# Conv module of a two-layer trunk: nine convolution blocks on TensorE, grouped layer-norm statistics, an ordered layer norm, and a queue of their own for the modulations' loads

## The chip, the cores and the metric

One core of one Trainium2 chip. The metric is the device time of one execution in microseconds, as the median of several runs. PE is TensorE, DVE VectorE, ACT ScalarE, POOL GpSimd, SP SyncE, which only issues transfers here.

## What is computed

A residual stream x of 256 tokens by 2048 goes through two layers. Layer 0 has a convolution module as its token mixer, layer 1 gated linear attention; each layer then has a feed-forward part with a short convolution. Every part is wrapped in norms and in shift, scale and gate that a product of the conditioning vector c with a 2048 x 12288 matrix gives ("modulations", adaLN):

```python
c_act = silu(c)
for i in range(2):
    shift_m, scale_m, gate_m, shift_f, scale_f, gate_f = split(c_act @ ada_w[i] + ada_b[i])
    h = rms_norm(x, norm_g[i, 0]) * (1 + scale_m) + shift_m
    y = conv_module(h) if i == 0 else gla(h)
    x = x + gate_m * rms_norm(y, norm_g[i, 1])
    h = rms_norm(x, norm_g[i, 2]) * (1 + scale_f) + shift_f
    x = x + gate_f * rms_norm(conv_ffn(h), norm_g[i, 3])

def conv_module(h):
    a, gate = split(h @ w_in)                       # 2048 -> 2 x 2048
    z = causal_dwconv(a * sigmoid(gate), dw_w) + dw_b   # 31 taps, each channel by itself
    z = silu(layer_norm(z, ln_g, ln_b))             # over the 2048 channels
    return z @ w_out
```

The change lies in layer 0's convolution module, the "first stage".

## The kernel before

All large products are taken in a split form: a weight block's high part is a cast on ACT (L121), its low part a subtraction on DVE (L123), and PE takes three products (high by high, low by high, high by low). Weights come as tiles of 1 MiB ("raw"), by a class `Stream`: a list of items in a fixed order, loaded ahead on SP's queue (`load`, L92 to L99) into a pool of four buffers. The adaLN items of layer 0 that are marked early go through a second pool of four buffers, `cols`, but in the same list and the same queue, so that a load whose buffer is still in use holds up all that stand behind it on SP.

An adaLN item is of one of two kinds. A *column* item goes to PE (`ada_col`): 512 of the inputs against 512 of the outputs, four narrow products a tile (L364) into an accumulator `ada`; when it is full, DVE transposes it (L371) and PE sums the four partial rows (`adas`, L378), and DVE adds the bias (L381). A *row* item goes to DVE (`ada_row`, L350): one multiply-and-reduce of a 128 x 2048 tile with the vector `cb`, about 2.28 us.

The first stage (`conv_mixer`, L597 on) runs in four parts.

- *Start.* The tokens x, the vector and the parameters `pr` are loaded, the shift and scale of the first norm come as column items of half width ("adah"), and the normed tokens are transposed.
- *cin.* The 16 blocks of 128 channels of a and of gate, in six steps (L742 to L762, products L756 to L758), 32 weight items. `gather` (L658) makes a * sigmoid(gate) of a block and puts it into one of two lists.
- *Convolution.* Eight blocks go to DVE (`taps_dve`, 30 instructions a block, L685), and eight to PE (PE_BLOCKS, `taps_pe`): 16 narrow products `ps_late` (L713) that shift the block, four copies on ACT (L715), and 32 narrow products `ps_conv` (L730) with diagonal matrices `zt` that DVE (L724, half of them) and ACT (the other half) build. As a block is finished it enters the layer norm's statistics: a product with a 128 x 128 matrix of ones for the mean (`mean_add`, L644), and, once 12 blocks give a first mean, its squares less that mean (L631, L632) by another such product (`squares`, L633). The rest of cin and the column items lie between these.
- *Layer norm and cout.* From the statistics DVE and ACT make the mean `mu` and 1/deviation `r_ln` (L778 to L786); every block is centered (L789), multiplied (L792), passed through silu (L793) and split (L424, L425) into `uc`. cout then takes 2048 columns in four blocks of 512: 96 products each (L522 to L524), the gate's multiplication (`y`, L583) at each block's end. Between its products stand column items, and between its low parts row items, by two tables (COLS_COUT, ROWS_COUT: how many at each weight item). The gate goes through DRAM to be spread over the partitions: `gate_rows` writes 2048 single numbers (`row`, L508) and reads them back four times (`gs`, L512), on POOL's queue.

The order of instructions on each engine is fixed when the program is built: the framework's scheduler places an instruction when its inputs are expected, by priorities, and an engine then runs its list in order. The change moves many instructions on all engines in the first stage; from the feed-forward part of layer 0 on the order stays.

Of the kernel before, what the change touches and what calls it, by code (L numbers as in the profile page):

```python
# [13 lines left out]
P = 128  # L14
# [13 lines left out]
PE_BLOCKS = (5, 7, 9, 11, 12, 13, 14, 15)  # L28
# [6 lines left out]
COLS_CONV = 16  # L35
# [11 lines left out]
COLS_COUT = (0, 0, 0, 1), (1, 1, 1, 1), (1, 1, 0, 0), (0, 0, 0, 0)  # L47
# [6 lines left out]
C_TAP = C_AB + 2 * 6 * KT  # L54
C_DWB = C_TAP
# [9 lines left out]
class Stream:  # L65
# [26 lines left out]
    def load(self, upto):  # L92
        while self.loaded < min(upto, len(self.items)):
            it = self.items[self.loaded]
            pool = self.cols if it["early"] else self.raw
            r = pool.tile([P, 2048], F32, tag="raw", name=f"raw{self.loaded}")
            self.nc.sync.dma_start(out=r[:, : it["n"]], in_=it["src"])
            self.raws[self.loaded] = r
            self.loaded += 1  # L99
# [91 lines left out]
def trunk_kernel(ctx: ExitStack, tc: tile.TileContext, x, cvec, ccol, adar, adac, adah, par, taps, wgate,  # L191
# [14 lines left out]
    nc.sync.dma_start(out=cc, in_=ccol)  # L206
    ones = const.tile([P, P], F32, tag="ones", name="ones")
# [4 lines left out]
    G.memset(onec, 1.0)  # L212

# [4 lines left out]
    pr = const.tile([P, NPAR], F32, tag="pr", name="pr")  # L218
# [70 lines left out]
    early_cols = list(cols[:COLS_CONV])  # L289
    fillc(COLS_CONV)  # L290
# [55 lines left out]

    def ada_row(key, r):

        _, l, m, k = key
        V.tensor_tensor_reduce(out=r, in0=r, in1=cb, scale=1.0, scalar=0.0, op0=ALU.mult, op1=ALU.add,  # L350
                               accum_out=mod[l, m][:, k : k + 1])

    def ada_col(key, r):
# [8 lines left out]
        for j in range(per):  # L362
            kt = per * i + j
            nc.tensor.matmul(ps[32 * (j % 4) : 32 * (j % 4) + 32], cz[:, kt], r[:, j * n : (j + 1) * n],  # L364
                             start=kt < 4, stop=kt >= KT - 4, tile_position=(0, 32 * (j % 4)))
        if i == KT // per - 1:

            trs = []
            for h in range(0, n, T):
                tr = small.tile([P, T], F32, tag="sq", name=f"adat{l}{m}{k0}{h}", bufs=3)  # L370
                V.transpose(out=tr, in_=ps[:, h : h + T])  # L371
                trs.append(tr.rearrange("p (c a i) -> p c a i", a=4, i=32))

            def sums():
                pt = apool["sums"](f"adas{l}{m}{k0}")
                for c, tr in enumerate(trs):
                    for a in range(4):
                        nc.tensor.matmul(pt[32 * a : 32 * a + 32, 2 * c : 2 * c + 2], mask32, tr[:, :, a, 0],  # L378
                                         start=True, stop=True, tile_position=(0, 32 * a))
# [122 lines left out]
    def gate_rows(l, which, gate, room=None):  # L502
# [4 lines left out]
        with nc.allow_non_contiguous_dma("2048 numbers"):  # L507
            G.dma_start(out=row.rearrange("k p -> p k"), in_=mod[l, gate])  # L508
        gs = []
        for c in range(4):  # L510
            g = room[c].rearrange("p (a b) -> p a b", b=P) if room else hpool.tile([P, 4, P], F32, tag="h", name=f"g{l}{which}{c}")
            G.dma_start(out=g, in_=row[4 * c : 4 * c + 4].unsqueeze(0).to_broadcast([P, 4, P]))  # L512
# [3 lines left out]
    def token_products(pv, t, parts, act, kt, nk):  # L516
# [7 lines left out]
        nc.tensor.matmul(pv, al, wh, start=False, stop=kt == nk - 1)  # L524
# [47 lines left out]
    def proj_out(name, act, l, which, gate, room=None):  # L572
        ss = new_sums(f"y{l}{which}")
        ys, dg, gs = {}, {}, []
        for c in range(4):

            def each(t, pv):
                if not gs:
                    gs.extend(gate_rows(l, which, gate, room))
# [17 lines left out]
    def conv_mixer(l):  # L597
        with early as cx:
            st.ahead = 8
            cm = cx.enter_context(tc.tile_pool(name="cm", bufs=2))  # L600
            tp = cm.tile([P, KT * (CW + 32)], F32, tag="tp", name="tp", bufs=1)
# [8 lines left out]
            on_dve, on_pe, ready, order = [], [], [], []  # L610
# [14 lines left out]

            def squares(j):
                n = len(squared)
                if n == 0:
                    acc["v"] = psum1.tile([P, T], F32, tag="acc", name="acc_v")
                sq = small.tile([P, T], F32, tag="sq", name=f"sq{j}", bufs=3)  # L630
                V.tensor_sub(sq, zs[j], mean_a)  # L631
                A.activation(sq, sq, AF.Square)  # L632
                nc.tensor.matmul(acc["v"], ones, sq, start=n == 0, stop=n == KT - 1)  # L633
                squared.append(j)
# [3 lines left out]
            def mean_add(j):  # L638


                n = len(added)
                if n in (0, NA):
                    acc["m"] = (psum1 if n == 0 else pp["ps"]).tile([P, 2 * T], F32, tag="acc" if n == 0 else "ps", name=f"acc_m{n}")[:, :T]
                nc.tensor.matmul(acc["m"], ones, zs[j], start=n in (0, NA), stop=n in (NA - 1, KT - 1))  # L644
                added.append(j)
                if n == NA - 1:
                    A.activation(mean_a, acc["m"], AF.Copy, scale=1.0 / (NA * P))
                    V.tensor_scalar_mul(part_a, mean_a, NA / KT - 1.0)
                if n >= NA - 1:
                    for i in added[len(squared) :]:  # L650
                        squares(i)

            def tap(j, s):

                c = j * CW + CW - 1 - s
                return tp[:, c : c + 1]

            def gather(j, ps, last):  # L658
# [7 lines left out]
                if last:  # L666
# [5 lines left out]
                    if j in PE_BLOCKS:  # L672
                        on_pe.append((j, zp, z))
# [27 lines left out]
            def taps_pe():  # L701


                while on_pe:
                    j, zc, z = on_pe.pop(0)
# [12 lines left out]
                    c0 = KT * CW + j * 32  # L718
                    w = tp[:, c0 : c0 + 32].rearrange("p (j a) -> p a j", a=8)
# [13 lines left out]
                    A.activation(z, ps, AF.Identity, bias=pc(C_DWB + j))  # L733
# [6 lines left out]
            A.dma_start(out=cb, in_=cvec.to_broadcast([P, D]))  # L740
# [23 lines left out]
            for step in range(1000):  # L764
                if step < len(early_cols):
# [372 lines left out]
```

## Time and profile before

| | us |
|---|---|
| runs | 2373.4, 2375.62, 2379.9 (median 2375.62) |
| profiled execution | 2376.87 |
| its span | 2375.2 |
| PE busy in the span | 2318.7 |
| first cin product | 29.6 |
| last product of the layer norm's statistics | 352.3 |
| first cout product | 368.8 |
| end of cout's third column block | 440.7 |
| mean granted clock of PE | 0.992 |

A row of a table of windows gives start and end, the busy us of PE, of its weight loads (PEld), of DVE, ACT and POOL with the number of instructions, the clock granted to PE as a share of full speed, the mean busy share of the 16 DMA engines, and GB/s. A row of the timeline gives start, duration, engine, line, operation, output and input, and in brackets how long the engine stood idle before and what it waited for. A row of a grouped list gives the count, busy us in total, and ns of one. A row of waits gives us in total, times, longest.

### The profile page before, as it was taken

Reading aid. Unit: us, or ns where it says so; the run is one execution under the profiler, and the core shown is the slowest. Engines: PE = TensorE matmul, PEld = TensorE weight load, DVE = VectorE, ACT = ScalarE, POOL = GpSimd, SP = SyncE. Lnnn points to the kernel's source line nnn. Section 1 sums busy time; section 2 is a strip of 40 time slices with the busy share of each in tenths; the row PEclk is TensorE's granted clock in tenths of the full one; section 3 lists DMA queues with packets and bytes.
Section 4 is the critical chain, followed back from the end, with each engine's and each line's share of the span. In section 5 each row is a group of like instructions: output and inputs, shape, how many; then the busy total and the mean of one; then the engine's idle time right before and its main releaser. Section 6 shows DMA issues by size and latency. Waiting matters only on the chain.

```text
span 2375.2 us, 34238 instructions
## 1 busy us (share of the span) xinstructions
PE 2318.7 (98%) x13516; PEld 1955.8 (82%) x13516; DVE 1772.2 (75%) x2554; ACT 1212.4 (51%) x1909; POOL 16.8 (1%) x43
## 2 busy tenths in 40 slices
PE   6999998999999999999999999999999999999998
PEld 5888746788878888888878888888888888888886
DVE  3779998778878888888877877756887466645665
ACT  5334465555534554345565576655554455544543
POOL 0000000000000000000000000000000000000000
PEclk9999998999999999999999999999999999999999
DMA  9878778657799878988946756563778555555553
GB/s 387 344 311 322 299 222 309 265 216 276 291 310 348 303 279 316 362 288 298 345 174 258 283 216 227 168 227 121 286 280 275 193 190 193 189 185 196 193 199 121
DMA packets 86577, 609.30 MB, mean 257 GB/s; under 512 B 10064, under 2 KB 10128, under 8 KB 13456
## 3 DMA queue, kind: packets, MB, share of 16 engines
q1 hardware_dynamic: 84800, 601.84, 69.2%
q0 software_dynamic: 1472, 4.23, 0.6%
q8 instruction: 106, 1.74, 0.3%
q10 hardware_dynamic: 144, 1.05, 0.1%
q14 instruction: 55, 0.45, 0.1%
HBM read 604.94 MB, written 2.13 MB: 256 GB/s over the span
## 4 chain that ended last, share of the span: by engine, by line
PE 95%; DMA 2%; DVE 1%; ACT 1%; issue 0%; SPq 0%; DVEq 0%; ACTq 0%
PE ps_fb L410 14%; PE ps_fa L410 14%; PE ps_fa L412 7%; PE ps_fb L412 7%; PE ps_fo L524 7%; PE ps_fo L523 7%; PE ps_fo L522 6%; PE ps_cin L756 3%; PE ps_cin L758 3%; PE ps_r L410 2%; PE ps_cin L757 2%; PE ada L364 2%; PE ps_r L412 1%; PE ps_q L410 1%; PE ps_cout L522 1%; PE ps_k L410 1%
## 5 line engine op out<-in xcount | busy, mean ns | idle before, releaser
L123 DVE TENSOR_TENSOR lo<-raw,hi 128x1024 fp32r<-128x1024 f32 (+1 forms) x760 | 914.3, 1214 | 398.7 <-ACT hi L121 395.5
L121 ACT CAST hi<-raw 128x1024 fp32r<-128x1024 f32 (+1 forms) x760 | 784.9, 1042 | 807.4 <-PE ps_fa L410 195.4
L410 PE MATMUL ps_fa<-h,hi 128*128 128x512 f32 x1408 | 356.4, 393 | 0.4 <-ACT hn L486 0.4
L410 PE MATMUL ps_fb<-h,hi 128*128 128x512 f32 x1408 | 354.9, 392 | 0.0
L350 DVE CUSTOM_DVE_ANT_0 raw<-raw,cb 128x2048 f32<-128x2048 f32 x140 | 319.6, 2284 | 30.6 <-DMA raw<-in_adar 30.5
L410 PEld LDWEIGHTS ps_fa<-h,hi 128*128 128x128 f32 x1408 | 252.9, 189 | 45.7 <-DVE h L488 0.6
L410 PEld LDWEIGHTS ps_fb<-h,hi 128*128 128x128 f32 x1408 | 252.5, 189 | 44.2
L523 PE MATMUL ps_fo<-lo,u 128*128 128x512 f32 x704 | 274.6, 390 | 4.1 <-DVE lo L123 4.1
L524 PE MATMUL ps_fo<-hi,u 128*128 128x512 f32 x704 | 274.6, 390 | 0.0
L522 PE MATMUL ps_fo<-hi,u 128*128 128x512 f32 x704 | 273.7, 390 | 0.0
L412 PEld LDWEIGHTS ps_fa<-h,lo 128*128 128x128 f32 x1408 | 193.7, 190 | 15.1 <-DVE lo L123 0.5
L412 PEld LDWEIGHTS ps_fb<-h,lo 128*128 128x128 f32 x1408 | 193.7, 190 | 14.7
L412 PE MATMUL ps_fa<-h,lo 128*128 128x256 f32 x1408 | 198.3, 282 | 0.1
L412 PE MATMUL ps_fb<-h,lo 128*128 128x256 f32 x1408 | 198.2, 282 | 0.0
L523 PEld LDWEIGHTS ps_fo<-lo,u 128*128 128x128 f32 x704 | 132.6, 188 | 32.1 <-DVE lo L123 4.6
L756 PE MATMUL ps_cin<-h,hi 128*128 128x256 f32 x512 | 148.4, 293 | 7.3 <-ACT hi L121 7.2
L524 PEld LDWEIGHTS ps_fo<-hi,u 128*128 128x128 f32 x704 | 132.5, 188 | 27.7
L522 PEld LDWEIGHTS ps_fo<-hi,u 128*128 128x128 f32 x704 | 132.6, 188 | 27.1
L758 PE MATMUL ps_cin<-h,lo 128*128 128x256 f32 x512 | 145.2, 288 | 1.1 <-DVE lo L123 1.1
L757 PE MATMUL ps_cin<-h,hi 128*128 128x256 f32 x512 | 146.0, 287 | 0.0
L756 PEld LDWEIGHTS ps_cin<-h,hi 128*128 128x128 f32 x512 | 100.0, 196 | 21.5 <-ACT hi L121 11.8
L758 PEld LDWEIGHTS ps_cin<-h,lo 128*128 128x128 f32 x512 | 99.2, 196 | 3.2 <-issue 1.7
(240 smaller groups left out, 2697.9 us busy)
## 6 DMA issues: line engine op xcount, KB each, us to landing
raw<-in_fin SPq DMA_DIRECT2D x176, 1024.0 KB, 4.8
raw<-in_adar SPq DMA_DIRECT2D x140, 1024.0 KB, 5.6
raw<-in_fout SPq DMA_DIRECT2D x88, 1024.0 KB, 5.1
raw<-in_adac SPq DMA_DIRECT2D x44, 1024.0 KB, 5.8
raw<-in_gin SPq DMA_DIRECT2D x33, 1024.0 KB, 4.9
raw<-in_cin SPq DMA_DIRECT2D x32, 1024.0 KB, 11.1
raw<-in_cout SPq DMA_DIRECT2D x16, 1024.0 KB, 7.8
raw<-in_gv SPq DMA_DIRECT2D x16, 1024.0 KB, 4.8
```

The costliest lines, as they stand in the source:

```text
L121: nc.scalar.copy(hi[:, :w], r[:, s : s + w])
L123: nc.vector.tensor_sub(lo[:, :w], r[:, s : s + w], hi[:, :w].bitcast(F32))
L350: V.tensor_tensor_reduce(out=r, in0=r, in1=cb, scale=1.0, scalar=0.0, op0=ALU.mult, op1=ALU.add, accum_out=mod[l, m][:, k : k + 1])
L364: nc.tensor.matmul(ps[32 * (j % 4) : 32 * (j % 4) + 32], cz[:, kt], r[:, j * n : (j + 1) * n], start=kt < 4, stop=kt >= KT - 4, tile_posit ...
L410: nc.tensor.matmul(ps, hi(k * P), act[k], start=k == 0, stop=False)
L412: nc.tensor.matmul(ps[:, :T], lo(k * P), act[k][:, :T], start=False, stop=k == nk - 1)
L522: nc.tensor.matmul(pv, ah, wh, start=kt == 0, stop=False)
L523: nc.tensor.matmul(pv, ah, wl, start=False, stop=False)
L524: nc.tensor.matmul(pv, al, wh, start=False, stop=kt == nk - 1)
L756: nc.tensor.matmul(ps[:, b], hi(o), ah, start=k == 0, stop=False)
L757: nc.tensor.matmul(ps[:, b], hi(o), al, start=False, stop=False)
L758: nc.tensor.matmul(ps[:, b], lo(o), ah, start=False, stop=k == nk - 1)
```

## The change

The edits, all in the first stage, by theme:

- *Convolution.* Block 10 joins PE_BLOCKS, so nine blocks run on PE and seven on DVE; of every odd block DVE builds both halves of `zt`. The taps' table is half as large.
- *Statistics.* The first 12 blocks enter in groups of four: for each block of a group a product with 32 columns of the ones, at one of four column positions of PE, into `acc_p` (means) or `acc_q` (squares); when 12 are in, one full product folds the four partial rows (`acc_a`, and `acc_v<-mu`). The last four blocks keep the full products. The squares are written into the block's spent input instead of a pool of three tiles.
- *Layer norm.* DVE's instructions stand in a written-out line: r_ln, three centers, the reciprocal, and then for each block its multiplication, the low part of the block two before, and the center of the block three ahead. Silu's table is loaded behind the square root.
- *Column and row items.* Twelve column items instead of 16 stand in the loop of the convolution; four stand in the gap behind the last statistics product, and no other PE product of adaLN passes those places ("tok"). Cout's columns end later (COLS_COUT). Row items of layer 0 wait for the layer norm's last instruction ("ln"), transposes for the reciprocal ("r"). Row items of layer 0 are all early but those of the last modulation.
- *Gate.* The gate's row is written by ACT's queue inside the convolution loop, and read back by SP's ahead of cout.
- *Queues.* Early items from the sixth on are loaded by POOL's queue (`gpsimd`) instead of SP's. `pr` comes in two pieces, the first by ACT's queue at the program's start; `cb` moves from ACT's queue to SP's; tokens and adah items alternate. Silu's table is loaded at the start.

```diff
-PE_BLOCKS = (5, 7, 9, 11, 12, 13, 14, 15)
+PE_BLOCKS = (5, 7, 9, 10, 11, 12, 13, 14, 15)
-COLS_CONV = 16
+COLS_CONV = 12
-COLS_COUT = (0, 0, 0, 1), (1, 1, 1, 1), (1, 1, 0, 0), (0, 0, 0, 0)
+COLS_COUT = (0, 0, 0, 0), (0, 1, 0, 1), (0, 1, 0, 1), (0, 0, 0, 0)
 ROWS_COUT = (0, 0, 0, 4), (2, 1, 2, 1), (2, 1, 2, 1), (0, 0, 0, 0)
...
-            self.nc.sync.dma_start(out=r[:, : it["n"]], in_=it["src"])
+            (self.nc.gpsimd if it["early"] and self.loaded > 4 else self.nc.sync).dma_start(out=r[:, : it["n"]], in_=it["src"])
...
-        early = key[0] == "col" or key[:3] in (("row", 0, 0), ("row", 0, 3))
+        early = key[0] == "col" or key[:2] == ("row", 0) and key[2] != 5
...
+        with after("ln") if l == 0 else ExitStack():
             V.tensor_tensor_reduce(out=r, in0=r, in1=cb, ...)
...
+            with after("tok"):
                 nc.tensor.matmul(ps[32 * (j % 4) : 32 * (j % 4) + 32], cz[:, kt], r[:, j * n : (j + 1) * n], ...)
...
-                V.transpose(out=tr, in_=ps[:, h : h + T])
+                with after("r"), tc.high_priority(SPLIT_FIRST):
+                    V.transpose(out=tr, in_=ps[:, h : h + T])
...
-    st.load(1)
     for t in range(2):
+        st.load(t + 2)
         for c in range(4):
             nc.sync.dma_start(out=X[t][c], in_=x[t, :, c * 512 : (c + 1) * 512])
-    nc.sync.dma_start(out=pr, in_=par)
-    st.load(4)
+    st.load(5)
+    nc.sync.dma_start(out=cb, in_=cvec.to_broadcast([P, D]))
+    nc.sync.dma_start(out=pr[:, C_DWB:], in_=par[:, C_DWB:])
...
+            def sums(few, all_, n, tiles):
+                mm = None
+                for i, z in reversed(list(enumerate(tiles))):
+                    if n < NA:
+                        with tc.issue_after(mm.ins) if mm else ExitStack(), tc.high_priority(SPLIT_FIRST):
+                            mm = nc.tensor.matmul(acc[few][32 * i : 32 * i + 32], ones[:, :32], z, start=n == 0, stop=n == NA - 4,
+                                                  tile_position=(0, 32 * i))
+                    else:
+                        mm = nc.tensor.matmul(acc[all_], ones, z, start=all_ == "m" and n == NA, stop=n == KT - 1)
+                return mm
...
-                            if a == 0:
+                            if a == 0 or j % 2:
                                 V.tensor_mul(zt, ...)
...
-            for step in range(1000):
-                if step < len(early_cols):
-                    st.upto(("col",) + early_cols[step], False)
...
+            gap = early_cols[COLS_CONV:]
+            while len(squared) < KT:
+                if early_cols:
+                    st.upto(("col",) + early_cols.pop(0), False)
+                elif gate is None:
+                    gate = gate_out(l, 1, 2, A)
...
+                for j in range(3):
+                    center(j)
+                queue(V.reciprocal, r, r)
+                for j in range(KT):
+                    queue(V.tensor_mul, zs[j], zs[j], r)
+                    A.activation(zs[j], zs[j], AF.Silu, bias=pc(C_LNB + j), scale=pc(C_LNG + j))
+                    A.copy(us[j][:, :T], zs[j])
+                    low(j - 2)
+                    center(j + 3)
...
+            apool["tok"] = apool["sqs"]
+            st.upto(("col",) + gap[-1], False)
+            gs = gate_rows(l, 1, 2, nc.sync, gate, room)
```

How PE's list passes from the statistics to cout, first before (`acc_m` and `acc_v` are the statistics' products, `ada` and `adas` the column items' products and sums):

```order
L644 MATMUL acc_m_3717<-pair_509,ones 128x256
L378 MATMUL adas_3994<-adat_3830,mask_88 32x2 x4
L378 MATMUL adas_3994<-adat_3832,mask_88 32x2 x4
L364 MATMUL ada_4160<-raw_3711,cz 32x512
L633 MATMUL acc_v<-sq_3835,ones 128x256
L364 MATMUL ada_4160<-raw_3711,cz 32x512
L633 MATMUL acc_v<-sq_3870,ones 128x256
L633 MATMUL acc_v<-sq_3875,ones 128x256
L364 MATMUL ada_4160<-raw_3711,cz 32x512 x2
L364 MATMUL ada_4160<-raw_4082,cz 32x512 x4
L522 MATMUL ps_cout_0_3992<-hi_0_4006,uc_3910 128x512
```

and the same place of PE now:

```order
L657 MATMUL acc_m<-pair_630,ones 128x256
L657 MATMUL acc_v<-pair_483,ones 128x256
L657 MATMUL acc_v<-pair_630,ones 128x256
L373 MATMUL ada_3921<-raw_3141,cz 32x512 x4
L373 MATMUL ada_3921<-raw_3188,cz 32x512 x4
L373 MATMUL ada_3921<-raw_3252,cz 32x512 x4
L373 MATMUL ada_3921<-raw_3305,cz 32x512 x4
L389 MATMUL adas_3952<-adat_3938,mask_91 32x2 x4
L540 MATMUL ps_cout_0_3950<-hi_0_3964,uc_3822 128x512
```

Before, two column items straddle the last statistics products, the second of them loaded only then; now four stand behind them, in buffers that were filled during the loop.

DVE in the layer norm before (`pair` is a block, `mu` its center, `r_ln` the factor; ten more centers stand where the rows are left out, in two places):

```order
L783 SCALAR_TENSOR_TENSOR r_ln<-acc_v,part_a 128x256
L789 TENSOR_TENSOR pair_301<-pair_301,mu 128x256
L784 TENSOR_SCALAR r_ln<-r_ln 128x256
L789 TENSOR_TENSOR pair_316<-pair_316,mu 128x256
...
L789 TENSOR_TENSOR pair_509<-pair_509,mu 128x256
L786 RECIPROCAL r_ln<-r_ln 128x256
L789 TENSOR_TENSOR pair_524<-pair_524,mu 128x256
...
L792 TENSOR_TENSOR pair_301<-pair_301,r_ln 128x256
```

and now:

```order
L831 SCALAR_TENSOR_TENSOR r_ln<-acc_v,part_a 128x256
L831 TENSOR_SCALAR r_ln<-r_ln 128x256
L831 TENSOR_TENSOR pair_305<-pair_305,mu 128x256
L831 TENSOR_TENSOR pair_320<-pair_320,mu 128x256
L831 TENSOR_TENSOR pair_335<-pair_335,mu 128x256
L831 RECIPROCAL r_ln<-r_ln 128x256
L381 STREAM_TRANSPOSE adat_3938<-ada_3921 128x256
L831 TENSOR_TENSOR pair_305<-pair_305,r_ln 128x256
L831 TENSOR_TENSOR pair_350<-pair_350,mu 128x256
L831 TENSOR_TENSOR pair_320<-pair_320,r_ln 128x256
```

Three centers stand ahead of the first multiplication now, where all 16 did.

At the end of cout's third column block PE has now (before, the last column item stood at 168 of cout's 384 products and its sums at 192):

```order
L542 MATMUL ps_cout_0_4302<-hi_1024_4402,uc_3903 128x512
L373 MATMUL ada_4210<-raw_4220,cz 32x512 x4
L540 MATMUL ps_cout_1_4303<-hi_1024_4402,uc_3903 128x512
...
L542 MATMUL ps_cout_1_4303<-hi_1024_4402,uc_3908 128x512
L373 MATMUL ada_4210<-raw_4313,cz 32x512 x4
L389 MATMUL adas_4495<-adat_4484,mask_91 32x2 x4
L540 MATMUL ps_cout_0_4478<-hi_0_4438,uc_3822 128x512
```

and DVE ahead of the transposes that those sums read (ISA is the multiply-and-reduce of a row item):

```order
L358 ISA raw_4256,m_106<-raw_4256,cb 128x2048
L358 ISA m_106 128x1
L123 TENSOR_TENSOR lo_1024_4518<-raw_4394,hi_1024_4517 128x1024
L358 ISA raw_4260,m_106<-raw_4260,cb 128x2048
L358 ISA m_106 128x1
L358 ISA raw_4309,m_106<-raw_4309,cb 128x2048
L358 ISA m_106 128x1
L601 TENSOR_TENSOR y_02_4470<-ps_cout_0_4302,gs_3943 128x512
L601 TENSOR_TENSOR y_12_4474<-ps_cout_1_4303,gs_3943 128x512
L123 TENSOR_TENSOR lo_0_4492<-raw_4353,hi_0_4491 128x2048
L381 STREAM_TRANSPOSE adat_4484<-ada_4210 128x256
```

The sums moved to the seam between the third and the fourth block, and the transposes stand behind the row items of the third.

More of the change, by code (lines that the diff above doesn't have):

```diff
@@ L53 @@
 C_AB = C_NG + 2 * 4 * KT
[L54 to L55 removed]
+C_DWB = C_AB + 2 * 6 * KT
 C_LNG = C_DWB + KT
@@ L212, in trunk_kernel @@
     G.memset(onec, 1.0)
+    table = const.tile([P, 1], F32, tag="table", name="table")
+    A.activation(table, onec, AF.Silu)
     cz = const.tile([P, KT, 32], F32, tag="cz", name="cz")
@@ L507, in gate_rows @@
         with nc.allow_non_contiguous_dma("2048 numbers"):
-            G.dma_start(out=row.rearrange("k p -> p k"), in_=mod[l, gate])
+            queue.dma_start(out=row.rearrange("k p -> p k"), in_=mod[l, gate])
+        return row
+    def gate_rows(l, which, gate, queue=G, row=None, room=None):
+        if row is None:
+            row = gate_out(l, which, gate, queue)
         gs = []
@@ L633, in squares @@
-                nc.tensor.matmul(acc["v"], ones, sq, start=n == 0, stop=n == KT - 1)
-                squared.append(j)
-            acc = {}
-            def mean_add(j):
-                n = len(added)
[L642 to L651, printed above, removed]
+                    nc.tensor.matmul(acc["v"], ones, mu, start=True, stop=False)
@@ L784, in conv_mixer @@
[L784 to L796 removed]
+            line = []
```

150 lines of the change are left out of this document (93 added, 57 removed).

## The prediction

> **What bounds the kernel now.** First the page: the span, the busy row and the clock.
>
> ```profile
> span 2375.2 us, 34238 instructions
> PE 2318.7 (98%) x13516; PEld 1955.8 (82%) x13516; DVE 1772.2 (75%) x2554; ACT 1212.4 (51%) x1909; POOL 16.8 (1%) x43
> ```
>
> PE (TensorE) is busy 98% of the span, so the change can gain only by PE work taken out of the first stage or by the few places where PE waits there. PE's waits in the first 440 us name those places:
>
> ```profile
> PE ada L364 <- DMA raw<-in_adac: 13.7, 1, 13.7
> ...
> PE ps_cin L756 <- ACT hi L121: 7.2, 4, 3.9
> ```
>
> The largest is the layer norm: 13.7 us. The windows (start:end, busy us of PE, weight load, DVE, ACT, POOL, then clock, DMA share, GB/s) show where the waits lie:
>
> ```profile
> 0.00:20.00 20.00, 4.81 (x32) 2.80 (x36) 1.79 (x9) 10.45 (x22) 1.50 (x12) 1.00 0.90 346
> 60.00:80.00 20.00, 17.82 (x141) 14.88 (x140) 15.76 (x18) 5.06 (x6) 0.00 (x0) 0.96 0.69 268
> 352.30:440.70 88.40, 74.24 (x334) 56.09 (x335) 78.30 (x110) 44.78 (x69) 2.15 (x4) 0.92 0.90 322
> ```
>
> Two things to see: in the first 20 us PE has little to do (4.81) while the DMA engines are full (share 0.90), and from the last statistics product (352.3) to the end of the third column block of cout (440.7) DVE is busy 78.30 of 88.4 us while PE is busy 74.24. There DVE is the fuller engine.
>
> The sum is made against the profiled execution, 2376.87 us; the median of the runs is 2375.62, 1.25 lower, and the forecast is given at the median.
>
> **(a) Start, 0 to the first cin product.** pr is split over two queues, Silu's table comes early, tp shrinks, cin0 goes ahead of cb, and later adah loads move to POOL's queue. All of these are transfers or short ACT work beside a DMA that is nearly full. At that window's 346 GB/s a load of 1.05 MB takes 3 us of it. Up to three adah loads (up to 9 us of the engines' time) can now run beside cin0 and x instead of behind them; against that, pr's rest and tp stand behind cin0. I take 0, bounds −5 (the time of two loads, less their issue) and +3 (one load more ahead of it).
>
> **(b) The loads' own queue.** In the timeline of SP, cin loads stood behind early loads that waited for a buffer:
>
> ```profile
> 61.82 0.33 SPq L97 DMA_DIRECT2D raw<-in_adac  x1
> 68.26 0.33 SPq L97 DMA_DIRECT2D raw<-in_adar  x1
> 68.68 0.79 SPq L97 DMA_DIRECT2D raw<-in_cin  x1
> ```
>
> In 61.82 to 68.68 no cin load was issued, though the DMA share of the window 60 to 80 is only 0.69. PE then waited:
>
> ```profile
> 78.07 0.39 PE L756 MATMUL ps_cin<-h,hi 128*128 128x256 f32 x1 [2.07 <-ACT hi L121]
> 165.26 0.39 PE L756 MATMUL ps_cin<-h,hi 128*128 128x256 f32 x1 [0.78 <-ACT hi L121]
> 166.21 0.39 PE L756 MATMUL ps_cin<-h,hi 128*128 128x256 f32 x1 [0.45 <-ACT hi L121]
> 167.62 0.58 PE L758 MATMUL ps_cin<-h,lo 128*128 128x256 f32 x1 [0.90 <-DVE lo L123]
> ```
>
> and ran slowly behind each wait:
>
> ```profile
> 78.00:80.00 2.00, 1.83 (x8) 1.50 (x9) 1.95 (x2) 0.96 (x2) 0.00 (x0) 0.64 1.01 426
> 80.00:82.00 2.00, 2.00 (x11) 2.00 (x11) 0.54 (x2) 0.00 (x0) 0.00 (x0) 0.51 1.02 434
> 168.00:170.00 2.00, 2.00 (x11) 2.00 (x11) 0.70 (x1) 0.00 (x0) 0.00 (x0) 0.50 1.02 430
> ```
>
> First place: 2.07 idle + (1 − 0.64) × 2 + (1 − 0.51) × 2 = 3.8 us. Second: 0.78 + 0.45 + 0.90 = 2.1, and a like loss of clock, 1.7: 3.8. Together 7.6. With early loads in POOL's queue, a cin load waits only for its own buffer. But the DMA share is 1.01 in these windows: early loads take their share of full engines in either queue, so part of the lateness stays. I take −5.5 (all of the second, about half of the first), bounds −8 and 0. The row above shows 0.51 within four microseconds of a wait of 2.07 us. The Trainium skill, "TensorE: Matmul & The Clock Gate", section "Why this matters for your kernels", warns of gaps of over about 3 us; by that rule the two clock terms (1.7 each) would be nothing and (b) at most 4.2. Here a shorter wait has cost clock, and the measurement decides.
>
> **(c) PE's work up to the last statistics product.** In the chain of waits, in order of time, PE's pieces follow one another here without a gap (315.74 + 3.16, then 318.89 + 0.86, then 319.75), so instructions count at their price:
>
> ```profile
> 315.74 3.16 PE ps_conv L730 x56
> 318.89 0.86 PE ada L364 x8
> 319.75 1.92 PE ps_late L713 x32
> 330.67 1.49 PE acc_v L633 x6
> ```
>
> (Two records are one fp32 product.) Block 10 on PE adds 16 ps_late, 1.92, and 32 ps_conv, 3.16 × 64/56 = 3.6: +5.5. Statistics of the first 12 blocks: 24 full products by 1.49/3 = 0.50 go, 12.0; 6 groups of four narrow products come, which run beside each other as ps_late's do (1.92/16 × 4 = 0.48), 2.9, and two folds by 0.50: −8.1. Of the adaLN column items 17 stood before the last statistics product and 12 do now; five by 0.86: −4.3, moved behind it (see d). Tail: each of the last blocks must pass ACT and DVE before its own square, as before; half a microsecond for the second fold: +0.5. Sum −6.4. DVE must keep pace: it loses 30 tap instructions of block 10 and takes 7 zt halves or so:
>
> ```profile
> L685 DVE SCALAR_TENSOR_TENSOR pair<-pair,tp 128x240 f32<-128x240 f32 x6 | 2.6, 464 | 0.0
> L724 DVE TENSOR_TENSOR zt<-tp,mask 128x512 f32<-128x512 f32 x7 | 4.7, 678 | 0.0
> ```
>
> −30 × 2.6/6 + 7 × 0.68 = −8 us, so it is not later than before. Bounds −9 (all waits of the taps' end go too) and −2 (DVE's taps end the stage and only 2 us of the 8 count).
>
> **(d) Layer norm.** Before, from the last statistics product to the first cout product:
>
> ```profile
> 351.16 1.13 PE L633 MATMUL acc_v<-sq,ones 128*128 128x256 f32 x4
> 352.40 0.42 DVE L783 SCALAR_TENSOR_TENSOR r_ln<-acc_v,part_a 128x256 f32<-128x256 f32 x1
> ...
> 356.64 1.75 DVE L786 RECIPROCAL r_ln<-r_ln 128x256 f32<-128x256 f32 x1
> 359.91 3.43 DVE L792 TENSOR_TENSOR pair<-pair,r_ln 128x256 f32<-128x256 f32 x10
> 366.96 1.94 PE L364 MATMUL ada<-raw,cz 128*32 128x512 f32 x8 [13.69 <-DMA raw<-in_adac]
> 368.83 0.80 PE L522 MATMUL ps_cout<-hi,uc 128*128 128x512 f32 x1
> ...
> 372.51 0.40 PE L522 MATMUL ps_cout<-hi,uc 128*128 128x512 f32 x1
> ...
> 439.21 0.39 PE L522 MATMUL ps_cout<-hi,uc 128*128 128x512 f32 x1
> ...
> 441.02 0.39 PE L524 MATMUL ps_cout<-hi,uc 128*128 128x512 f32 x1
> ```
>
> That is 368.83 − 352.3 = 16.5 us, and products at half speed until about 372.5: nine in 3.68 us where the eight steps from 439.21 to 441.02 take 0.226 each (some 1.8 us lost). The column load that PE waited for fell together with the gate's row (the DMA issues of 330 to 400 us: KB, median us to landing) in a window of full DMA and few bytes:
>
> ```profile
> 356.00:360.00 4.00, 0.00 (x0) 0.00 (x0) 4.00 (x10) 0.25 (x1) 0.00 (x0) 0.81 0.87 66
> ...
> raw<-in_adar SPq DMA_DIRECT2D x8, 1024.0 KB, 5.5
> gs<-row POOLq DMA_DIRECT2D x4, 256.0 KB, 7.2
> row<-m POOLq DMA_DIRECT2D x1, 8.0 KB, 16.7
> ```
>
> That row, 2048 single numbers, now goes out on ACT's queue inside the conv loop, several blocks before t0, where four early loads lie ready ahead of PE: I take 0 for it, and if that cover is gone it costs there the 13.7 that it cost here. DVE did 11 centers ahead of the reciprocal and ten multiplications ahead of the first low part. Now: r_ln 0.42, maximum 0.29, square root 0.51, reciprocal 1.75, one multiplication 0.34, silu and cast about 0.9, latencies 1 to 2: 5.5 to 6 us, in which PE has the four gap items (4 × 0.86 = 3.4). So cout starts t0 + 6, where t0 is the last statistics product: some 10.5 us earlier, 12 with the clock.
>
> **(e) What DVE gives back in cout.** The adaLN columns that stood at 168 of cout's 384 products end now at 288, and behind them, ahead of the fourth column block, PE has the sums of their transposes. DVE reaches those transposes behind 15 row items, 24 low parts of 1024, all of the layer norm, six y and one low part of 2048. By the groups from the last statistics product on:
>
> ```profile
> L350 DVE CUSTOM_DVE_ANT_0 raw<-raw,cb 128x2048 f32<-128x2048 f32 x14 | 31.7, 2283 | 0.0
> L123 DVE TENSOR_TENSOR lo<-raw,hi 128x1024 fp32r<-128x1024 f32 x22 | 26.4, 1221 | 7.8 <-ACT hi L121 7.7
> L425 DVE TENSOR_TENSOR uc<-pair,uc 128x256 fp32r<-128x256 f32 x16 | 5.9, 418 | 0.0
> L583 DVE TENSOR_TENSOR y<-ps_cout,gs 128x512 f32<-128x512 f32 x4 | 2.6, 683 | 0.0
> ```
>
> 15 × 31.7/14 = 34.0; 24 × 1.20 = 28.8; 48 × 5.9/16 = 17.7; 6 × 0.65 = 3.9; the wide low part as two of 1024, 2.4; reciprocal 1.75; accumulator reads, transposes and small ones 3.8: 92. The groups of a window overlap a little (those of 352.3 to 440.7 add to 83 where the window shows 78.30), so × 0.945: 87. With 2 us idle, and the sums after it, the fourth block starts at t0 + 89. PE is done with the third block at t0 + 6 + 3 × 96 × 0.226 + 4 × 0.86 = t0 + 75, so it waits some 14 us there and then runs slow as it did at 368.83 to 372.5 (+1.8). Before, that point was 440.7 = t0 + 88.4. So (d) and (e) together: 89 + 1.8 − 88.4 = **+2.5**: all that the layer norm gains is waited for again. Bounds: −8 (DVE is not what ends the wait; the first rival) and +6 (DVE idle 5 us between loads). From there on the instructions stand in the same order as before.
>
> Sum: 0 − 5.5 − 6.4 + 2.5 = −9.4. 2376.9 − 9.4 = 2367.5 in a profiled execution, **2366** at the median.
>
> **Rivals.**
>
> *DVE doesn't pace cout.* If its work up to the transposes takes under 80 us instead of 87, PE waits there only for its last column load, which is issued when the buffer of the one before is free, nine products (2 us) earlier, and lands in about 5.5 (the row loads' median, above). The fourth block starts at t0 + 75 + 5.5, and 1.5 of clock is lost, t0 + 82: (d, e) −6.4, total −18.3, **2357**; 2350 without any wait. Against it: the sum of 87.
>
> *The own queue gains nothing.* The DMA share of 1.01 in both waits says that bytes, not the queue, are late. Then (b) is 0, and at the start the adah loads only take bandwidth from cin0: +3. Sum +3 − 6.4 + 2.5 = −0.9, **2375**. For it: the full share; against it: 0.69 in the 20 us ahead of the first wait. The Trainium skill, "DMA: Bandwidth & Descriptors", section "Issuing engines are not separate DMA queues", says that loads from several engines run on the same 16 DMA engines and only issue time is saved. By that rule this rival would hold; the held cin load of 61.82 to 68.68 is issue time of the kind that it leaves to be saved.
>
> *Slower: POOL's loads are late.* In cout 15 rows and 4 columns go through four buffers in about 77 us (from t0 + 5 to t0 + 82), 4.05 us each, so 16 us for a buffer's turn, 2.3 of it use. If a load of 1 MB from POOL's queue takes more than 14 us, it sets the pace. The two POOL rows above are 7.2 for a quarter of the bytes and 16.7 for 8 KB (of single numbers). At 18 us a load: 19 × 20.3/4 = 96 instead of 77, +19; −5.5 − 6.4 + 2.5 + 19 = +9.6, **2385**. Against it: 7.2 is near what SP's loads take. The Trainium skill, "SBUF — State Buffer", section "SBUF: two separate sides", says that GpSimd-issued DMAs starve for descriptors while DVE holds the port that they share; DVE is busy nine tenths of cout. No run here shows it on a load of 1 MB.
>
> **How the numbers follow.** Forecast 0.55, first rival 0.12, own queue for nothing 0.21, POOL late 0.12. A measurement of this kernel tells about 0.3%, 7 us, from no change: faster is under 2368.5. Of the forecast's 0.55 three quarters lie there (its bounds at the start and in (b) reach beyond): 0.41 + 0.12 = 0.53 faster; 0.14 + 0.21 = 0.35 the same; 0.12 slower. The range takes in the first rival's 2357 with 3 us to spare for its last wait, 2354, and, above, the second with (c) at its weak bound (4.4 more), 2378; it leaves out most of POOL's case and the first rival without any wait.
>
> **What would show it.** Right: no wait of PE near 78 and 165 with SP's cin issues no longer behind buffers; the last statistics product at about 340 instead of 352; cout's first product 6 us behind it; a wait of some 14 us ahead of the fourth block, by PE on the transposes' results, and a clock of about 0.5 behind; DVE busy over 90% from t0 to there; the last cout product some 9 us earlier than before. Wrong: PE waiting in the conv loop for a column load, a first cin product later than 33 us, POOL's loads over 14 us, or PE passing the third block without a wait.

## The result: slower by 0.6%, and where the time went

The changed kernel takes 2392.89 us in the median (five runs, 2387.44 to 2394.30) against 2378.93 before (five runs); the ratio is 1.006, with a 95% interval of 1.0049 to 1.0071. The forecast was 2366, and its range ended at 2378. The profiled execution took 2394.3 us, 17.4 more than the one of before (2376.87); the median moved by 14.0.

The timelines of PE give the borders of the stages (us from the start of the span):

| | before | changed | difference of the step |
|---|---|---|---|
| first cin product | 29.6 | 29.5 | −0.1 |
| end of the last cin product | 266.6 | 272.9 | +6.4 |
| end of the last statistics product (t0) | 352.3 | 353.6 | −5.0 |
| first cout product | 368.8 | 359.3 | −10.8 |
| first product of cout's fourth block | 441.3 | 452.6 | |
| end of cout | 463.2 | 477.7 | +24.1 |
| end of the span | 2375.2 | 2392.6 | +2.9 |

So three of the steps went as drawn: the start (by luck, as shown below), the convolution with its statistics, and the layer norm. Two went the other way: cin lost 6.4 us where 5.5 were to be gained, and cout, which was to take some 13 us more, took 24.1 more. The page of the changed kernel, first its span and busy row:

```profile
span 2392.6 us, 34351 instructions
PE 2324.0 (97%) x13616; PEld 1963.0 (82%) x13616; DVE 1769.7 (74%) x2531; ACT 1200.5 (50%) x1836; POOL 53.8 (2%) x114
```

PE has 5 us more to do and waits some 12 us more. Its list of waits in the first 500 us:

```profile
PE ada L373 <- DMA raw<-in_adac: 13.9, 3, 6.8
PE adas L389 <- DVE adat L381: 10.4, 6, 5.1
PE ada L373 <- DMA raw<-in_adah: 7.2, 2, 6.7
PE ada L373 <- DVE adat L381: 6.4, 1, 6.4
PE ps_cin L800 <- ACT hi L121: 6.4, 2, 5.9
```

Before, one wait of 13.7 us for a column item's load stood in the layer norm. Now waits for column loads sum to 13.9, but they are three and lie elsewhere. The waits for transposes have grown to 10.4 from the row of before:

```profile
PE adas L378 <- DVE adat L371: 1.1, 2, 0.6
```

and a new row stands in the list, for a buffer that a transpose frees (6.4).

**The layer norm.** The timeline of all engines at t0:

```profile
353.54 3.64 PE L373 MATMUL ada<-raw,cz 128*32 128x512 f32 x32
354.15 0.42 DVE L831 SCALAR_TENSOR_TENSOR r_ln<-acc_v,part_a 128x256 f32<-128x256 f32 x1 [0.48 <-ACT part_a L847]
355.83 1.75 DVE L831 RECIPROCAL r_ln<-r_ln 128x256 f32<-128x256 f32 x1
358.85 0.41 ACT L861 CAST uc<-pair 128x256 fp32r<-128x256 f32 x1
359.31 0.52 PE L540 MATMUL ps_cout<-hi,uc 128*128 128x512 f32 x1 [1.13 <-ACT uc L861]
```

The four gap items fill PE for 3.64 us, and cout begins 5.7 us behind t0 (16.5 before). This part of the change works.

**Cout.** Behind it PE waits for column items, by the timeline of PE:

```profile
403.22 1.20 PE L373 MATMUL ada<-raw,cz 128*32 128x512 f32 x8 [3.46 <-DMA raw<-in_adac]
435.84 1.94 PE L373 MATMUL ada<-raw,cz 128*32 128x512 f32 x8 [3.62 <-DMA raw<-in_adac]
448.62 1.93 PE L373 MATMUL ada<-raw,cz 128*32 128x512 f32 x8 [6.81 <-DMA raw<-in_adac]
452.39 0.29 PE L389 MATMUL adas<-adat,mask 128*32 128x2 f32 x8 [1.83 <-DVE adat L381]
```

These are 15.7 us of waits, with slower products behind them (the clock is 0.62 in the window 440 to 460). The timeline of POOL shows when the loads were issued:

```profile
357.51 0.53 POOL L97 DMA_DIRECT2D raw<-in_adar  x1 [0.33 <-PE ada L373]
388.08 0.53 POOL L97 DMA_DIRECT2D raw<-in_adar  x1 [30.04 <-DVE m L358]
390.29 0.53 POOL L97 DMA_DIRECT2D raw<-in_adar  x1 [1.68 <-DVE m L358]
394.77 0.53 POOL L97 DMA_DIRECT2D raw<-in_adac  x1 [3.95 <-DVE m L358]
...
422.20 0.53 POOL L97 DMA_DIRECT2D raw<-in_adac  x1 [1.14 <-DVE m L358]
...
439.87 0.53 POOL L97 DMA_DIRECT2D raw<-in_adac  x1 [1.23 <-DVE m L358]
```

Four row loads take the four early buffers at 355 to 358 us and hold them until DVE reaches the first row item at 385.5. For 30 us POOL can issue nothing. Two more rows stand ahead of the first column item, which is issued at 394.8, when PE is 5 us from needing it. The windows show what the pause costs:

```profile
358.00:388.00 30.00, 28.87 (x134) 23.37 (x135) 28.24 (x60) 25.25 (x47) 0.04 (x1) 0.94 0.63 238
388.00:400.00 12.00, 11.76 (x52) 9.39 (x51) 12.00 (x11) 4.65 (x6) 2.12 (x4) 1.00 1.00 387
400.00:440.00 40.00, 33.16 (x139) 23.93 (x140) 30.71 (x29) 11.27 (x14) 5.43 (x11) 0.89 1.00 410
```

The DMA engines are used at 0.63 for 30 us and then full for 52, while PE waits. DVE is busy 30.71 of the 40 us from 400: it isn't what bounds cout.

**Cin.** Its waits, in the timeline of PE, lie at other places than the two of before (78 and 165), which are gone:

```profile
22.00 1.94 PE L373 MATMUL ada<-raw,cz 128*32 128x256 f32 x16 [6.41 <-DVE adat L381]
44.04 0.58 PE L800 MATMUL ps_cin<-h,hi 128*128 128x256 f32 x1 [5.86 <-ACT hi L121]
93.22 0.29 PE L389 MATMUL adas<-adat,mask 128*32 128x2 f32 x8 [5.13 <-DVE adat L381]
```

The wait at 44 us is for a weight of cin itself, whose load landed late, by the timeline of ACT:

```profile
42.94 1.99 ACT L121 CAST hi<-raw 128x1024 fp32r<-128x1024 f32 x2 [7.36 <-DMA raw<-in_cin]
```

### The profile page after: what moved, and what is told of

It is laid out like the page before. It is cut to its first block, busy times and chain, and to the rows that moved or that the text cites. A ratio compares the mean times of both kernels' runs of the same rounds, so it can differ in the third digit from the quotient of the medians.

```text
span 2392.6 us, 34351 instructions
## 1 busy us (share of the span) xinstructions
PE 2324.0 (97%) x13616; PEld 1963.0 (82%) x13616; DVE 1769.7 (74%) x2531; ACT 1200.5 (50%) x1836; POOL 53.8 (2%) x114
## 4 chain that ended last, share of the span: by engine, by line
PE 78%; DVE 1%; DMA 1%; ACT 1%; issue 0%; DVEq 0%; ACTq 0%
PE ps_fb L422 14%; PE ps_fa L422 13%; PE ps_fa L424 7%; PE ps_fb L424 7%; PE ps_fo L541 6%; PE ps_fo L542 6%; PE ps_fo L540 6%; PE ps_r L422 2%; PE ps_r L424 1%; PE ps_q L422 1%; PE ps_v L540 1%; PE ps_gout L541 1%; PE ps_gout L540 1%; PE ps_gout L542 1%; PE ps_v L542 1%; PE ps_v L541 1%
## 5 line engine op out<-in xcount | busy, mean ns | idle before, releaser
L540 PEld LDWEIGHTS ps_fo<-hi,u 128*128 128x128 f32 x704 | 132.5, 188 | 27.6
L800 PEld LDWEIGHTS ps_cin<-h,hi 128*128 128x128 f32 x512 | 99.4, 194 | 23.6 <-issue 10.9
L801 PEld LDWEIGHTS ps_cin<-h,hi 128*128 128x128 f32 x512 | 99.4, 194 | 0.8 <-DVE pair L711 0.8
```

Source lines behind the costliest of these rows:

```text
L540: nc.tensor.matmul(pv, ah, wh, start=kt == 0, stop=False)
L800: nc.tensor.matmul(ps[:, b], hi(o), ah, start=k == 0, stop=False)
L801: nc.tensor.matmul(ps[:, b], hi(o), al, start=False, stop=False)
```

## The experiments

The theory after the result, A: *place, not speed*. In cin a queue of its own takes its share of DMA engines that are full anyway, from loads that PE needs sooner; in cout the column items stand in one list and four buffers behind row items that DVE reaches late. Rival B: a load that POOL issues is slow in itself. Rival C: cin is late for another reason. Rival D, the prediction's step: DVE's work in cout sets its end. Ratios are to the kernel before on the same chip (2377.4 to 2377.8 in the medians there).

### All early loads on SP's queue again (e1_sp)

```diff
-            (self.nc.gpsimd if it["early"] and self.loaded > 4 else self.nc.sync).dma_start(out=r[:, : it["n"]], in_=it["src"])
+            self.nc.sync.dma_start(out=r[:, : it["n"]], in_=it["src"])
```

> All early loads go back to SP's queue, everything else as changed. Theory A (place in the list: in cout the four column items stand in one list and four buffers behind row items that DVE reaches late; in cin a queue of its own takes DMA time from cin's loads): the last cin product ends at 266 to 268 us instead of 272.9, and cout does not get shorter (118 us changed; 110 to 130, since cout's weights now stand behind the held row loads). Theory B (a load issued by POOL is slow in itself): cin as in A, and cout falls to 94 to 105 us. The sum: A 2380 to 2400, B 2365 to 2375.

Measured: 2381.68 us, ratio 1.0018 (1.0005 to 1.0031). The first cin product comes at 26.4, the last ends at 261.2, better than A said: 11.8 earlier than changed and 5.4 earlier than before. Cout takes 113.5 us. Its longest wait, in the timeline of PE, is now for a weight:

```profile
423.81 0.79 PE L540 MATMUL ps_cout<-hi,uc 128*128 128x512 f32 x1 [10.06 <-ACT hi L121]
436.84 0.29 PE L389 MATMUL adas<-adat,mask 128*32 128x2 f32 x8 [3.52 <-DVE adat L381]
```

Without any load by POOL cout is only 5 us shorter, and B's 94 to 105 did not come. But here cout's weights stand behind the held row loads, which lengthens cout too, so this run alone does not rule B out for cout; e3_cols and e5_both do. Cin's loss is the queue's.

### Split: SP's queue up to the last cin item, POOL's behind it (e2_split)

```diff
+        self.own = self.index["cin", len(STEPS) - 1, len(ADA[-1]) - 1]
...
-            (self.nc.gpsimd if it["early"] and self.loaded > 4 else self.nc.sync).dma_start(out=r[:, : it["n"]], in_=it["src"])
+            (self.nc.gpsimd if it["early"] and self.loaded > self.own else self.nc.sync).dma_start(out=r[:, : it["n"]], in_=it["src"])
```

> Early loads go by SP's queue up to the last cin item, and by POOL's from there on. Theory A: the last cin product ends at 266 to 268 us instead of 272.9, the layer norm's gap stays 5.7 us, cout stays at 118 us: 2385 to 2388. Theory B: the same in cin, and cout as long. Rival C (the cin stage is late for another reason, such as block 10 or the longer list of transposes): the last cin product stays at 272 to 274, 2392.

Measured: 2379.39 us, ratio 1.0013 (1.0003 to 1.0023); the profiled execution, 2386.33, was the longest of its ten. First cin product 26.0, last 263.6, the gap 5.8, cout 119.6. A holds in each part (cin gains more than it said), C falls, and the gain in the median is larger than A's 5 to 8. In cin the two waits of before are back, 2.22 us at 75.1 and 0.77 at 161.2: they come with the shared queue. So the queue of its own did remove them, and paid more elsewhere. The windows of 30 to 100 us, first of the changed kernel:

```profile
30.00:100.00 70.00, 59.01 (x491) 52.17 (x490) 44.85 (x59) 30.00 (x39) 6.35 (x12) 0.90 0.94 385
```

and of this one:

```profile
30.00:100.00 70.00, 66.66 (x581) 57.36 (x581) 48.80 (x68) 31.64 (x43) 0.00 (x0) 1.00 0.93 380
```

The same bytes (385 and 380 GB/s at a share of 0.94 and 0.93), and PE is busy 7.7 us less, at a lower clock (0.90 instead of 1.00).

### Only the start's items back on SP (e11_start)

```diff
-            (self.nc.gpsimd if it["early"] and self.loaded > 4 else self.nc.sync).dma_start(out=r[:, : it["n"]], in_=it["src"])
+            (self.nc.gpsimd if it["early"] and self.loaded > 10 else self.nc.sync).dma_start(out=r[:, : it["n"]], in_=it["src"])
```

> The changed kernel with the eight half-wide items of the start back on SP's queue, and all later early items on POOL's as changed. Theory A in two parts: the first cin product comes at 25 to 27 us instead of 29.5 (POOL's loads took the DMA from the tokens), and the stage still loses some 3 to 6 us behind it, its last product at 268 to 271. If all of the lateness comes from the start: 262 to 265. If the start has no part in it: 272 to 274. Cout stays at 118 us in each: 2382 to 2392.

Measured: 2387.21 us, ratio 1.0039 (1.0027 to 1.0050). First cin product 25.0, last 267.6, cout 118.7. A in both parts: of the 9.4 us between the changed kernel (272.9) and the split one (263.6) some 5 go at the start and 4 behind it. At the start POOL issues two adah loads at 9.0 and 11.5 us beside the tokens' second half, and DVE's first transposes, which stand behind the tokens' statistics, come at 21.50 (16.98 in e1_sp). PE waits for them: the 6.41 above. Behind the start the wait is now for a column load, in PE's timeline of this run:

```profile
67.25 1.93 PE L373 MATMUL ada<-raw,cz 128*32 128x512 f32 x8 [5.04 <-DMA raw<-in_adac]
```

### Cout's column items ahead of its row items (e3_cols)

```diff
-COLS_COUT = (0, 0, 0, 0), (0, 1, 0, 1), (0, 1, 0, 1), (0, 0, 0, 0)
+COLS_COUT = (1, 1, 1, 1), (0, 0, 0, 0), (0, 0, 0, 0), (0, 0, 0, 0)
```

> The four column items of cout go into its first column block, ahead of the row items, by the table of columns alone. Theory A: PE waits under 5 us for column loads in cout, the fourth column block no longer waits for transposes, cout takes 94 to 98 us instead of 118: 2368 to 2373. Theory B: POOL's loads stay late, cout stays above 110 us: 2385 or more. The theory of the prediction (DVE's work ahead of the transposes sets the end of the third block): the transposes stand earlier, so cout falls as in A; DVE must then be busy over 95% of cout.

Measured: 2381.85 us, ratio 1.0018 (1.0009 to 1.0028): 11 us better than changed, by one line of a table. PE waits for no column load in cout. But cout takes 105.0, not 94 to 98: the first three blocks run through, and the fourth takes 32 us instead of 22, with waits that neither theory had named (between the two, filler products, `clock` of L569, take another 3.5 us):

```profile
440.47 0.50 PE L540 MATMUL ps_cout<-hi,uc 128*128 128x512 f32 x1 [3.22 <-ACT hi L121]
446.30 0.51 PE L541 MATMUL ps_cout<-lo,uc 128*128 128x512 f32 x1 [1.27 <-DVE lo L123]
```

B falls: the column items still come by POOL's queue, and cout is below B's 110. DVE is busy 92.20 of cout's 104.95 us, 88%, where the prediction's step asked for over 95%.

### Both (e5_both)

The edits of the split queue and of the columns together.

> SP's queue for early loads up to the last cin item, POOL's behind it, and cout's four column items in the first column block. Theory A: both gains add, the last cin product at 266 to 268 and cout 94 to 98 us: 2361 to 2367, faster than both kernels. Theory B: only cin's gain, 2385 to 2388.

Measured: 2371.93 us, ratio 0.9974 (0.9964 to 0.9983). The last cin product ends at 264.7, t0 is 346.2, cout takes 107.3. Faster than both kernels, though not by what was expected, and again the fourth block is the reason: 425.1 to 459.4, 34 us. B had said 2385 or more.

### Without the spare buffers (e6_spare)

Two weights of the fourth block are split not in the ordinary pool but in the early items' four buffers (`st.spare`), which before came free early. On top of e5_both:

```diff
-            for i in (1, 2):
-                st.spare["cout", 3, i] = st.cols, "raw", D
```

> The version with the split queue and cout's columns first, without the spare: two weights of cout's fourth block are then split in the ordinary pool instead of in all four buffers of the early items. Theory A (the fourth block waits for those buffers, which the last row items hold): the fourth block takes 23 to 27 us instead of 34, cout 96 to 100 instead of 107: 2362 to 2365. Rival D (DVE's work in cout, rows and low parts together, sets its end): the fourth block stays at 31 us or more, 2370 to 2373.

Measured: 2366.09 us, ratio 0.9951 (0.9936 to 0.9966), just above A's 2362 to 2365. The fourth block takes 26.4 us (423.5 to 450.0), cout 99.5. A holds: the fourth block waited for buffers that the last row items held. The timeline of ACT in e5_both shows it, where the cast of a wide weight part waits for a row item's end on DVE:

```profile
431.75 3.82 ACT L122 CAST hi<-raw 128x2048 fp32r<-128x2048 f32 x3 [2.55 <-DVE m L359]
```

D falls for the fourth block, since DVE's work is the same; over the first three blocks DVE is busy 95% in both runs. The windows of this run:

```profile
380.00:400.00 20.00, 20.00 (x103) 16.04 (x102) 18.84 (x21) 9.81 (x13) 2.12 (x5) 1.00 1.01 419
400.00:420.00 20.00, 20.00 (x90) 16.57 (x89) 19.69 (x18) 8.96 (x12) 2.11 (x4) 1.00 1.01 422
420.00:440.00 20.00, 18.10 (x72) 14.02 (x71) 17.82 (x19) 6.56 (x9) 1.06 (x2) 0.92 0.85 344
```

PE is busy throughout 380 to 420, with DVE and the DMA engines nearly full beside it: three resources end close to each other here, and what remains is a wait of 1.87 us for a low part at 435.9.

### Row items moved into the fourth block (e7_rows)

On top of e6_spare:

```diff
-ROWS_COUT = (0, 0, 0, 4), (2, 1, 2, 1), (2, 1, 2, 1), (0, 0, 0, 0)
+ROWS_COUT = (0, 0, 0, 2), (1, 1, 1, 1), (1, 1, 1, 1), (2, 2, 2, 0)
```

> As the run without the spare, and six of cout's sixteen row items move into its fourth block. Theory A: little more than without the spare, 2360 to 2365, cout 94 to 99. Rival D: this is the one that helps, cout falls to 93 to 97 here and stays above 104 without the spare alone.

Measured: 2365.80 us, ratio 0.9950 (0.9935 to 0.9965); cout 99.3. Nothing over e6_spare (and just above A's 2360 to 2365); D had said 93 to 97 for cout.

### All on one queue, with the rest mended (e10_one)

e6_spare with every early load on SP's queue:

```diff
-            (self.nc.gpsimd if it["early"] and self.loaded > self.own else self.nc.sync).dma_start(out=r[:, : it["n"]], in_=it["src"])
+            self.nc.sync.dma_start(out=r[:, : it["n"]], in_=it["src"])
```

> The fastest version so far (split queue, cout's columns first, no spare: 2366 us), with all early loads on SP's queue, in cout as well. If a queue of its own helps where row loads wait for DVE (cout's weights no longer stand behind them): cout takes 104 us or more instead of 99.5, 2371 or more. If the queue gives nothing there (bytes, not order, bound the loads): cout 98 to 101, 2364 to 2368.

Measured: 2374.63 us, ratio 0.9990 (0.9978 to 1.0001); cout 105.6. The queue of its own pays here, some 8 us, where row loads wait for DVE and cout's weights would stand behind them.

### Block 10 back on DVE (e8_blocks)

On top of e5_both:

```diff
-PE_BLOCKS = (5, 7, 9, 10, 11, 12, 13, 14, 15)
+PE_BLOCKS = (5, 7, 9, 11, 12, 13, 14, 15)
```

> The version with the split queue and cout's columns first, with block 10 back on DVE (eight blocks on PE). If PE sets the end of the convolution loop: the last statistics product comes 3 to 5.5 us earlier than 346.2 (the price of block 10 on PE, 5.5), 2366 to 2369. If DVE's taps set it: 0 to 8 us later, 2372 to 2380.

Measured: 2376.70 us, ratio 0.9991 (0.9982 to 1.0001); t0 at 349.0, 2.7 later than in e5_both, though PE has 5.5 us less to do. DVE's taps (L732) and the squares behind them (L674) end the loop then, by the list of PE's waits from 262 to 352 us:

```profile
PE acc_m L658 <- DVE pair L732: 3.6, 1, 3.6
PE acc_v L658 <- ACT pair L674: 3.6, 2, 2.6
```

Nine blocks on PE are better than eight here: e5_both took 2371.93.

### One column item in the gap (e9_gap)

On top of e5_both:

```diff
-COLS_CONV = 12
+COLS_CONV = 15
...
-    early_cols = list(cols[: COLS_CONV + 4])
-    fillc(COLS_CONV + 4)
+    early_cols = list(cols[: COLS_CONV + 1])
+    fillc(COLS_CONV + 1)
```

> The version with the split queue and cout's columns first, with one column item in the gap behind the statistics instead of four (fifteen in the loop). If the four gap items only fill a wait of PE: the loop ends 2.6 us later, the gap stays at 5.8 us, and cout's own columns can be loaded in the loop, so its first block takes 23 to 25 us instead of 27: about the same, 2370 to 2374. If the gap items lengthen the gap: it falls to under 4.5 us, and the run is 1 to 3 us faster.

Measured: 2374.77 us, ratio 0.9989 (0.9979 to 0.9998). The loop ends 2.5 us later (348.8) and the gap stays at 6.0, so the four items fill a wait, as expected; but cout's first block is hardly shorter (27.2 us from its first product to the end of its last, 27.7 in e5_both), a miss: its length does not come from late loads.

## Why the prediction was wrong

- **(a) Start: the number right, by luck.** 0 was forecast and −0.1 measured. The start's other edits do bring 3.6 (26.0 in e2_split instead of 29.6), and POOL's loads, which the sum had put on the side of the gain, take it back. Both lay within the bounds named.
- **(b) The loads' own queue: −5.5 forecast, +6.4 measured. A failed step.** The waits at 78 and 165 went, as drawn. What was wrong was to count only them: with the DMA full (0.94 from 30 to 100 us), loads issued sooner are bytes taken from others. The sum had the fact ("early loads take their share of full engines in either queue") and used it only to shrink the gain, with a bound of 0. It needed to ask which load comes later. The Trainium skill, "DMA: Bandwidth & Descriptors", section "Issuing engines are not separate DMA queues", says that transfers started by several engines run on the same 16 DMA engines. The runs here agree: nearly the same share and GB/s with one queue and with two.
- **(c) Convolution and statistics: −6.4 forecast, −5.0 measured. Right.** Four gaps of PE in the loop, under 1 us each and 2.4 together, are more than the missing 1.4. e8_blocks bears out that DVE would have been late without block 10's move.
- **(d) Layer norm: 16.5 to 5.7 us, −10.8; forecast −10.5. Right**, and so was the cover for the gate's row: between 305 and 315 us the DMA engines are at 1.07 and 0.72 with 100 and 36 GB/s, and PE waits for no load there. The windows:

```profile
305.00:310.00 5.00, 4.91 (x85) 2.50 (x81) 5.00 (x14) 1.95 (x5) 0.53 (x1) 1.00 1.07 100
310.00:315.00 5.00, 4.10 (x56) 2.57 (x52) 4.63 (x12) 0.41 (x2) 0.53 (x1) 1.00 0.72 36
```

- **(e) Cout: t0 + 89 forecast for the fourth block, t0 + 99 measured. The failed step with the largest share.** The size of DVE's work up to the transposes was right: 87 us forecast, 86.10 measured, but in 98.3 us:

```profile
353.60:451.90 98.30, 81.19 (x369) 58.83 (x368) 86.10 (x117) 49.24 (x76) 10.61 (x20) 0.90 0.86 344
```

  DVE itself idles 12 us there, 8.9 of them for high parts whose weights or buffers come late. The step "DVE paces cout" took an engine that is 88% busy for the bound. The bound was the list: columns behind rows in four buffers. The tables of the change showed both (the first four rows at the last weight of cout's first block, the first column in the second block), and the first rival spoke of "its last column load" as the only one that could be late. It also took 5.5 us for that load from the row loads; the same list of 330 to 400 us has 7.9 for the column loads. That three of the four would be was missed, because a buffer's turn was priced at an even 4 us over 77, where it is 30 us of nothing and then a rush.
- **The rivals.** "POOL's loads are late" had the sign and 2385, with a mechanism that was wrong in the main: it had each load slow. The list of DMA issues of the first 480 us shows nearly the same landing time for a column item by either queue, first before:

```profile
raw<-in_adac SPq DMA_DIRECT2D x44, 1024.0 KB, 5.8
```

  and changed:

```profile
raw<-in_adac POOLq DMA_DIRECT2D x44, 1024.0 KB, 5.9
```

  But only 4 of these 44 lie in cout, where the DMA is full. There (354 to 478 us) the list has

```profile
raw<-in_adar POOLq DMA_DIRECT2D x16, 1024.0 KB, 9.2
raw<-in_adac POOLq DMA_DIRECT2D x4, 1024.0 KB, 10.5
```

  and in e1_sp, all by SP (348 to 463 us),

```profile
raw<-in_adar SPq DMA_DIRECT2D x12, 1024.0 KB, 7.0
raw<-in_adac SPq DMA_DIRECT2D x4, 1024.0 KB, 9.1
```

  So the loads are issued late, and then land slowly by either queue; the third column load, issued at 422.20, let PE go on only at 435.84. What makes POOL's 1 to 2 us slower stays open. The Trainium skill, "SBUF — State Buffer", section "SBUF: two separate sides", warns that DVE can starve the descriptors of POOL's loads. No idle DMA engine shows that here: their share is 1.00 from 388 to 440 us, with DVE busy 42.7 of these 52 us. "The own queue gains nothing" was nearer for cin, and still on the wrong side.

What stays open: some 5 us of cout in e6_spare (99.5 against 94.4 before). Its first block takes 27.6 us against 24.4 and has four column items where one stood; its fourth takes 26.4 against 21.9, of which the wait of 1.87 us is one part. And the 2.9 us that the changed kernel loses behind the first stage, of which a wait of 1.6 us in the second layer, which the profile of before doesn't have, is the only part found. In e6_spare it is 4.2 us, most of it right behind cout: the feed-forward part's first product comes 12.8 us after cout's end instead of 9.5.

## What to carry to other kernels

A queue of its own removes waits behind a held load, but not bytes: where the DMA engines are full, ask which load gets later. Items that share an in-order list and a few buffers move at the pace of the one that is picked up last, so the ones that the bounding engine needs go first; here one line of a table was worth 11 us. In e6_spare (0.9951) the profiled span is 9.0 us shorter than before: 7.6 are gained up to t0 and 10.7 in the layer norm, 5.1 are lost in cout and 4.2 behind it. An engine busy 88% of a stretch isn't its bound until what ends its idle time has been read.

## What the runs showed of the hardware

- A load of 1 MB issued by POOL keeps POOL busy for 0.53 us. A column load lands after 5.9 us in the median of the first 480 us (5.8 by SP before); in cout, with the DMA full, after 10.5 (9.1 by SP in e1_sp).
- While 2048 single numbers are written to DRAM, the DMA engines show a high share for about 10 us (1.07 and 0.72) with only 100 and 36 GB/s moved, and column loads land late. In the changed kernel, by the list of DMA issues of 305 to 315 us:

```profile
raw<-in_adac POOLq DMA_DIRECT2D x2, 1024.0 KB, 13.0
```

  Before, a column load that ran beside them landed 13.7 us after PE wanted it; inside the loop, with four loads lying ready, PE waited for none.
